# First attention unit's scores and softmax among the last column's products; mask copies by ScalarE

## The chip, the core and the metric

The kernel runs on one core of one Trainium2 chip, alone. The metric is the device time of one execution in microseconds (us). Five engines work side by side, each through its own instruction queue in order: TensorE (PE; its weight loads are listed as PEld), VectorE (DVE), ScalarE (ACT), GpSimd (POOL) and SyncE (SP), which here only issues DMAs. Where two of them share a buffer, one waits for the other.

## What is computed

One step of a hybrid layer. A prompt of 1024 tokens and 8 sample tokens go through one input projection, whose columns feed three groups: a sparse attention group (NSA: compressed, selected and window branches, 8 query heads, 2 key heads), an RWKV-7 recurrence, and cross-attention into 256 memory rows. The parts that matter here:

```
q_raw, kv_raw, g_raw, z_nsa, u_rw, z_rw, q_mem, z_mem = split_in(rms_norm(hp, ln_g[l]) @ w_in[l])
...
s = jnp.where(mask, s.astype(jnp.float32), -jnp.inf)     # masked_softmax
p = jnp.exp(s - m)
return p / jnp.maximum(jnp.sum(p, axis=-1, keepdims=True), 1e-30)
...
cat = jnp.concatenate([o_nsa * silu(z_nsa), o_rw * silu(z_rw), o_mem * silu(z_mem)], axis=-1)
return cat @ w_out
```

With 16 selected blocks of 64 rows in a prompt of 1024, the selected branch is full causal attention; the window branch is limited to 512 rows.

## The kernel before

**Three phases** follow each other in `run`. Phase 1 makes the transposed input `h` (as two parts, high and low, for precision: every product is three matmuls), multiplies it with the columns of `w_in`, 128 columns at a time, and fills the gaps of the RWKV recurrence with those products. Phase 2 does the prompt's attention, with the sample's work between. Phase 3 is the output projection.

**The end of phase 1.** `columns` makes one column block after another, each in two halves of the tokens (H = 0 in pieces of 256 and 264 columns of PSUM, then H = 1 with 512). Eight steps of three matmuls (`p_pr`) make a piece. The last blocks are gate columns: `do_z` takes tanh on ScalarE and a product on VectorE into `zt`, and SP stores it to `z_d`. While these products run, `mix` places other work between them: `keys_ahead` (keys transposed into `kh`, `kl`, and the queries of tile 7), `prompt_cmp` (the compressed keys) and `mem_turn` (memory rows), until `mem_product` multiplies the memory rows (`p_mo`, stored as `mkv`). The last column block comes behind `mem_product`.

**`prompt_cmp`** loads a table of masks, `c_am`, into slot 4 of a pool of eight 4 KB slots, and GpSimd copies it into `bmask` and `cmask` (L1313 to L1318). Then the rows `px` are transposed on TensorE (`p_xt`) and copied by ScalarE into `pxt` (L1340). `pxt` lies in slot 4 too. So the first `pxt` copy cannot start before the last copy out of `c_am` is done. In GpSimd's queue the copies stand behind two DMA issues of the RWKV output (`y_d<-y_c`, L1040).

**Phase 2** goes over units (i, g, hp): query tile i from 7 down, key head g, a pair of heads hp. `attn_scores` makes, for each branch b and head h, the scores on TensorE (`p_s`, two PSUM buffers), adds the mask and takes the maximum in one VectorE instruction (L1478, writes `p` and `nm`), exponentiates on ScalarE (L1485, with the sum), takes a reciprocal on VectorE (`fac`), and scales by it and by the gate on GpSimd (L1516). `attn_turn` transposes the weights `p` (`p_pT`, copied to `pt` by ScalarE and VectorE in turn), and `attn_out` multiplies them with the values (`p_o`). Unit n's transposes and products stand on TensorE with the scores of the units ahead and with pieces of other work: `attn_cmp` (`p_sc`, `pcq`) and `q_stack` (`qhl`, `p_q`).

**What sets the order.** Instructions are recorded in the order of the code, and a scheduler orders them by engine with priorities; work recorded under `high_priority` can move ahead. `InOrder` chains TensorE's matmuls, with a new chain at the start of each phase. A buffer of a pool that lies over an older one waits for the older one's readers: the tiles `p` of phase 2 lie over tiles of phase 1.

Of the kernel before, what the change touches and what calls it, by code (L numbers as in the profile page):

```python
# [10 lines left out]
F32 = mybir.dt.float32  # L11
# [10 lines left out]
NS = 8  # L22
# [25 lines left out]
def bc(ap, shape):  # L48
    return ap.to_broadcast(shape)
# [64 lines left out]
class Step:  # L114
# [357 lines left out]
    def phase1(self):  # L472
# [9 lines left out]
        with ExitStack() as ctx:  # L482
            P = lambda name, bufs, **k: ctx.enter_context(tc.tile_pool(name=name, bufs=bufs, reuse_waits="tile", **k))
            self.small = P("small", 2)
            self.hp = P("hp", 1)
            self.ev = P("ev", 1)
            self.wr = P("wr", 2)
            self.wp = P("wp", 2)
            rctx = ctx.enter_context(ExitStack())
            PR = lambda name, bufs: rctx.enter_context(tc.tile_pool(name=name, bufs=bufs, reuse_waits="tile"))  # L490
# [5 lines left out]
            self.rp = R("rp", 1)  # L496
            self.ppr = P("ppr", 3, space=PSUM)
            self.ptr = P("ptr", 2, space=PSUM)
            self.pw = P("pw", 3, space=PSUM)
            self.hi, self.lo = ([], []), ([], [])  # L500
# [807 lines left out]
    def prompt_cmp(self):  # L1308
# [3 lines left out]
        nc.sync.dma_start(am[:], I["c_at"][:, 0:504])  # L1312
        G.memset(self.bmask[:], 0.0)  # L1313
        G.memset(self.one[:], 1.0)
        G.tensor_copy(self.bmask[:, 0:128], am[:, 128:256])
        G.tensor_copy(self.bmask[:, 1024:1152], am[:, 0:128])
# [136 lines left out]
    def attn_scores(self, i, g, hp, Ps):  # L1453
# [16 lines left out]
        def weigh(ps, h, b, c0):  # L1470
            x, w = Ps[h, b][:, :n1 - c0], n1 - c0
            if b == 1 and split:
                m = bass.AP(tensor=self.bmask.tensor, offset=self.bmask.offset, ap=[self.bmask.ap[0], [832, 2], [1, 320]])
                halves = lambda t: t.rearrange("p (a c) -> p a c", a=2)
            else:
                m, halves = self.bmask[:, 1152 - w:1152], lambda t: t
            def mask():
                return V.tensor_tensor_reduce(halves(x), halves(ps), m, -1.0, 3.0e38, op0=OP.add, op1=OP.min,  # L1478
                                              accum_out=nm[:, h, b:b + 1])

            self.in_turn(mask) if begin else mask()
            if (hp, b, h) in ((0, 1, 1), (1, 0, 0), (1, 1, 0)):
                while self.held:
                    self.held.pop()()
            e = A.activation(x, x, AF.Exp, scale=-1.0, bias=nm[:, h, b:b + 1], accum_out=sm[:, h, b:b + 1])  # L1485
            if (i, g, hp, b, h) == (7, 0, 1, 0, 0):
                self.exp = e

        begin = (i, g) == (7, 0)
        f = self.small.tile([128, 2, 2], F32, name="fac")  # L1490
        hd = 4 * g + 2 * hp
        for b in range(2):
            c0 = w0 if b else 0
            for h in range(2):
                Ps[h, b] = self.pp.tile([128, 1024 if b == 0 else 640], F32, name="p", tag=f"p{b}")
# [15 lines left out]
            def scale(b=b, w=n1 - c0):  # L1511
                recip = lambda: V.reciprocal(f[:, :, b], sm[:, :, b])  # L1512
                self.in_turn(recip) if begin else recip()
                for h in range(2):
                    x = Ps[h, b][:, :w]
                    nc.gpsimd.tensor_scalar(x, x, f[:, h, b:b + 1], gate[:, hd + h, 1 + b:2 + b], op0=OP.mult, op1=OP.mult)  # L1516

            if begin and (hp, b) != (1, 1):
                self.held.append(scale)
            else:  # L1520
                scale()
# [135 lines left out]
    def phase2(self):  # L1657
        tc, nc, I, O = self.tc, self.nc, self.I, self.O
        with ExitStack() as ctx:
# [4 lines left out]
            self.tk = self.wk  # L1664
            self.pS = P("pS", 2, space=PSUM)
            self.pT = P("pT", 3, space=PSUM)
            self.pO = P("pO", 1, space=PSUM)
            self.pM = Tag(self.pT, "t")
# [11 lines left out]
            P = [{} for _ in units]  # L1680
            self.done, self.tail, self.jobs, self.unit = set(), [], [], 0
            self.held, self.mask = [], None
            gens = self.query_tasks(), self.tile_tasks(), self.sample_tasks(), self.sample_rest()
# [53 lines left out]
            next(start)  # L1737
            step(0)
            for _ in start:
                pass  # L1740
            for j, (n, a, b) in enumerate(groups):
                i, g, hp = units[n]
                self.unit = n
                if a == 0:
                    left = sum(1 for m, _, _ in groups if m == n)
                    if (g, hp) == (0, 0):
                        rate = RATE[i]
                        if i < 7:
# [3 lines left out]
                        if i == 7:  # L1752
                            self.load_z(6)
                        if i > 0 and i < 7:
                            self.load_z(i - 1)
                    pieces = sum(4 if units[m][0] >= 4 else 2 for m in ahead(n))
                    nxt = chain(*(scores(m) for m in ahead(n)))
# [27 lines left out]
    def sample_tables(self):  # L1785
# [6 lines left out]
        for d in range(2):  # L1792
            for s in range(2):
                V.tensor_tensor(t[:, 0:3, d, s], g[:, :, s], bc(cos, [NS, 3, 32]), op=OP.mult)
                V.tensor_tensor(t[:, 4:7, d, s], g[:, :, 1 - s], bc(sin, [NS, 3, 32]), op=OP.mult)
            A.activation(rows[:NS, 384 + 64 * d:448 + 64 * d], self.gains[:NS, 4, :], AF.Copy)
        V.tensor_scalar(t[:, 4:7, :, 0], t[:, 4:7, :, 0], -1.0, None, op0=OP.mult)
        return rows[:NS, 0:896].rearrange("p (k c) -> p k c", k=7)

    def sample_setup(self):  # L1800
# [784 lines left out]
```

## Time and profile before

| | us |
|---|---|
| three timed runs | 929.98, 934.21, 935.8 (median 934.21) |
| the profiled execution's own time | 932.48 |
| its span, first to last instruction | 930.7 |
| TensorE busy in the span | 890.9 (96%) |
| VectorE, ScalarE, GpSimd busy | 645.9, 439.6, 189.9 |

The profile is of one execution. A row of the timeline gives the start, the duration, the engine, the line of the kernel, the operation with output and inputs, and in brackets how long the engine was idle before it and what ended that. A duration overlaps with the next instruction's, since instructions are pipelined: the step from one start to the next is the cost. A row of a table by windows gives, for each engine, the busy time in that stretch, then the granted TensorE clock (1.00 is full), the share of time that the DMA engines were busy, and GB/s.

### The profile page before, as it was taken

How to read it: one execution, taken by the hardware profiler on the slowest of the kernel's cores; microseconds unless marked ns; L12 is line 12 of the kernel's file. 1: busy time of each engine (PE TensorE's matmuls, PEld its weight loads, DVE VectorE, ACT ScalarE, POOL GpSimd, SP SyncE). 2: the span in 40 equal slices, each digit the busy share in tenths (PEclk: the TensorE clock that was granted, in tenths of full speed). 3: DMA queues.
4: the chain of work that ended last, by engine and by line, in shares of the span. 5: the costliest groups of instructions: out<-in, count | busy, mean ns of one | idle time of the engine just before them, and what ended most of it. 6: DMA issues, size and time to landing. Idle time of an engine off the chain costs nothing.

```text
span 930.7 us, 24648 instructions
## 1 busy us (share of the span) xinstructions
PE 890.9 (96%) x9839; PEld 756.6 (81%) x9839; DVE 645.9 (69%) x2002; ACT 439.6 (47%) x1003; POOL 189.9 (20%) x283
## 2 busy tenths in 40 slices
PE   8999999999999999988998999999999998999998
PEld 8998888977878788757986788888887877887976
DVE  7768679954777459945556876666778986548454
ACT  7654324232443233223536577667567776324211
POOL 2000000000000000001103544454445766112010
PEclk9999999999999999999999999999999999999999
DMA  8521314141321204524738413332130027986561
GB/s 281 133 74 35 105 36 121 51 115 48 89 82 53 76 14 133 134 84 121 183 102 231 137 59 120 106 117 66 33 87 13 29 81 209 307 259 213 177 236 48
DMA packets 128298, 107.01 MB, mean 115 GB/s; under 512 B 26385, under 2 KB 113112, under 8 KB 128056
## 3 DMA queue, kind: packets, MB, share of 16 engines
q1 hardware_dynamic: 123096, 93.43, 34.3%
q0 software_dynamic: 3296, 10.75, 3.3%
q8 instruction: 78, 1.28, 0.6%
q10 hardware_dynamic: 1792, 1.26, 0.4%
q14 instruction: 36, 0.29, 0.1%
HBM read 84.72 MB, written 22.78 MB: 116 GB/s over the span
## 4 chain that ended last, share of the span: by engine, by line
PE 67%; DVE 18%; ACT 5%; issue 4%; DMA 3%; POOL 2%; SPq 1%; DVEq 0%; ACTq 0%; POOLq 0%
PE p_pr L86 24%; PE p_out L86 8%; PE p_s L86 5%; PE p_o L86 5%; PE p_pT L86 4%; PE p_pr L306 2%; PE p_hid L86 2%; ACT p L1485 2%; DVE p L1478 2%; DMA wraw<-in_w_in_dram 2%; PE p_it L86 1%; DVE wlo L283 1%; PE p_tk L86 1%; PE p_iy L86 1%; DVE pt L1446 1%
## 5 line engine op out<-in xcount | busy, mean ns | idle before, releaser
L86 PE MATMUL p_pr<-h,whi 128*128 128x512 f32 (+2 forms) x1168 | 282.2, 335 | 2.0 <-DVE zt L318 2.0
L86 PEld LDWEIGHTS p_pr<-h,whi 128*128 128x128 f32 x1168 | 190.2, 190 | 22.1 <-issue 2.8
L86 PE MATMUL p_pr<-h,wlo 128*128 128x512 f32 (+2 forms) x584 | 188.9, 326 | 1.1 <-DVE wlo L283 1.1
L1516 POOL TENSOR_SCALAR p<-p,fac,gates 128x640 f32<-128x640 f32 (+7 forms) x128 | 104.2, 826 | 89.4 <-DVE fac L1512 56.0
L86 PEld LDWEIGHTS p_pr<-h,wlo 128*128 128x128 f32 x584 | 109.8, 189 | 11.3 <-DVE wlo L283 1.5
L1485 ACT ACTIVATE p<-p,nm 128x640 f32<-128x640 f32 (+7 forms) x128 | 93.1, 729 | 40.7 <-DVE nm L1478 37.4
L86 PE MATMUL p_pT<-ident,p 128*128 128x128 f32 x528 | 71.9, 279 | 8.8 <-DVE pt L1446 4.0
L1104 POOL MEMSET w2d<- 128x128 f32 x1 | 0.2, 205 | 376.8 <-PE p_iy L86 376.8
L86 PEld LDWEIGHTS p_pT<-ident,p 128*128 128x128 f32 x528 | 56.6, 140 | 21.6 <-issue 5.9
L86 PE MATMUL p_o<-pt,vs 128*64 128x128 f32 x1056 | 67.9, 276 | 0.4 <-DVE cat L1554 0.4
L86 PE MATMUL p_s<-kh,qs 128*128 128x512 f32 (+3 forms) x191 | 64.8, 352 | 1.8 <-DVE nm L1478 1.6
L1478 DVE CUSTOM_DVE_ANT_0 p<-p_s,bmask 128x512 f32<-128x512 f32 (+7 forms) x96 | 60.6, 661 | 7.6 <-PE p_s L86 6.1
L282 ACT ACTIVATE whi<-wraw 128x1024 fp32r<-128x1024 f32 x34 | 36.0, 1059 | 62.3 <-PE p_pr L86 48.8
L86 PEld LDWEIGHTS p_o<-pt,vs 128*64 128x64 f32 x1056 | 57.0, 137 | 7.7 <-issue 4.2
L283 DVE TENSOR_TENSOR wlo<-wraw,whi 128x1024 fp32r<-128x1024 f32 x33 | 40.3, 1221 | 33.0 <-ACT whi L282 32.9
L86 PE MATMUL p_s<-kl,qs 128*128 128x512 f32 (+3 forms) x192 | 60.4, 334 | 0.0
L1446 DVE COPY pt<-p_pT 128x512 f32<-128x512 f32 (+1 forms) x72 | 48.2, 673 | 11.7 <-PE p_pT L86 11.5
L86 PE MATMUL p_out<-woh,chi 128*128 128x512 f32 x128 | 51.7, 404 | 0.0
L86 PE MATMUL p_out<-woh,clo 128*128 128x512 f32 x128 | 50.2, 392 | 0.4 <-DVE clo L2421 0.4
L86 PE MATMUL p_out<-wol,chi 128*128 128x512 f32 x128 | 49.9, 390 | 0.0
L1444 ACT ACTIVATE pt<-p_pT 128x512 f32<-128x512 f32 (+1 forms) x72 | 41.1, 577 | 14.2 <-PE p_pT L86 13.6
L86 PEld LDWEIGHTS p_s<-kh,qs 128*128 128x128 f32 x191 | 36.1, 189 | 5.5 <-DVE nm L1478 3.0
(546 smaller groups left out, 1779.5 us busy)
## 6 DMA issues: line engine op xcount, KB each, us to landing
wraw<-in_w_in_dram SPq DMA_DIRECT2D x34, 512.0 KB
pg<-in_c_pool_dram SPq DMA_DIRECT2D x32, 256.0 KB
pg<-in_c_pool_dram SPq DMA_DIRECT2D x48, 128.0 KB
x<-in_x_prompt_dram SPq DMA_DIRECT2D x8, 512.0 KB
z_d<-zt SPq DMA_DIRECT2D x16, 256.0 KB
cat<-z_d SPq DMA_DIRECT2D x8, 512.0 KB
xres<-in_x_prompt_dram POOLq DMA_DIRECT2D x16, 256.0 KB, 3.6
out_dram<-xres POOLq DMA_DIRECT2D x16, 256.0 KB, 3.0
```

The lines of the kernel that those rows point to most:

```text
L86: self.last = getattr(self.engine, op)(*a, **k)
L282: nc.scalar.activation(hi[:, :, :n], raw[:, :, :n], AF.Copy)
L283: (low or nc.vector).tensor_tensor(lo[:, :, :n], raw[:, :, :n], hi[:, :, :n].bitcast(F32), op=OP.subtract)
L306: self.last_mm = self.pe.matmul(ps[:m, :b - a], w[:, k, :m], h[k][:, a:b], start=(k == 0 and i == 0), stop=(k == 7 and i == 2))
L1104: nc.gpsimd.memset(w2d[:], 0.0)
L1444: nc.scalar.activation(pt[:, :n], ps[:, :n], AF.Copy)
L1446: nc.vector.tensor_copy(pt[:, :n], ps[:, :n])
L1478: return V.tensor_tensor_reduce(halves(x), halves(ps), m, -1.0, 3.0e38, op0=OP.add, op1=OP.min, accum_out=nm[:, h, b:b + 1])
L1485: e = A.activation(x, x, AF.Exp, scale=-1.0, bias=nm[:, h, b:b + 1], accum_out=sm[:, h, b:b + 1])
L1516: nc.gpsimd.tensor_scalar(x, x, f[:, h, b:b + 1], gate[:, hd + h, 1 + b:2 + b], op0=OP.mult, op1=OP.mult)
```

## The change

1. The copies from `c_am` into `bmask` and `cmask` go from GpSimd to ScalarE, and GpSimd clears only the columns of `bmask` that no copy writes.
2. `first_scores` runs the scores and softmax of unit 0, (7, 0, 0), inside the last column block, at the steps given by `AT`. Its PSUM buffers `pS` are opened once the buffers of `ptr` and `pw` are closed, and its four `p` tiles lie in slots 4, 5, 6 and 0, with maxima, sums and factors in unused columns of the tile in slot 6.
3. What follows from it: phase 2 starts with unit 1's scores, `cat6` is loaded at unit 1 (it lies in slot 6), the sample's tables and cleared tiles wait for unit 0's last reciprocal, exponential and scaling, unit 1's first scalings are held in other places, and the pool `ev` (with `zt`) is opened behind `wr` and `wp`.

```diff
+AT = (1, 5, 8, 11)
...
             self.hp = P("hp", 1)
-            self.ev = P("ev", 1)
             self.wr = P("wr", 2)
             self.wp = P("wp", 2)
+            self.ev = P("ev", 1)
...
-            self.ppr = P("ppr", 3, space=PSUM)
-            self.ptr = P("ptr", 2, space=PSUM)
-            self.pw = P("pw", 3, space=PSUM)
+            self.ppr = P("ppr", 3, space=PSUM, side="right")
+            pctx = ctx.enter_context(ExitStack())
+            PP = lambda name, bufs: pctx.enter_context(tc.tile_pool(name=name, bufs=bufs, reuse_waits="tile", space=PSUM))
+            self.ptr = PP("ptr", 2)
+            self.pw = PP("pw", 3)
...
-            self.mix(work, chain(self.columns(cols[EARLY:-1]), self.mem_product(), self.columns(cols[-1:])))
+            self.mix(work, chain(self.columns(cols[EARLY:-1]), self.mem_product()))
+            pctx.close()
+            self.pS = self.kctx.enter_context(tc.tile_pool(name="pS", bufs=2, reuse_waits="tile", space=PSUM))
+            self.first_scores(self.columns(cols[-1:]))
+
+    def first_scores(self, fill):
+
+        self.held, self.mask = [], None
+        self.P0 = {}
+        gen = self.attn_scores(7, 0, 0, self.P0)
+        for n, _ in enumerate(fill):
+            if n in AT:
+                next(gen, None)
+        for _ in gen:
+            pass
+        self.lasts = [x.ins for x in (self.r_last, self.e_last, self.g_last)]
...
-        G.memset(self.bmask[:], 0.0)
+        G.memset(self.bmask[:, 128:1024], 0.0)
         G.memset(self.one[:], 1.0)
-        G.tensor_copy(self.bmask[:, 0:128], am[:, 128:256])
-        G.tensor_copy(self.bmask[:, 1024:1152], am[:, 0:128])
+        A.activation(self.bmask[:, 0:128], am[:, 128:256], AF.Copy)
+        A.activation(self.bmask[:, 1024:1152], am[:, 0:128], AF.Copy)
         self.cmask = self.kt.tile([128, 248], F32R, name="cmask")
-        G.tensor_copy(self.cmask[:], am[:, 256:504])
+        A.activation(self.cmask[:], am[:, 256:504], AF.Copy)
...
+        early = (i, g, hp) == (7, 0, 0)
+        begin = (i, g, hp) == (7, 0, 1)
+        if early:
+            for (h, b), j in zip(((0, 0), (1, 0), (0, 1), (1, 1)), (4, 5, 6, 0)):
+                Ps[h, b] = self.slot(j, [128, 1024], F32, f"p{j}")
+            nm, sm, f = (Ps[0, 1][:, c:c + 4].rearrange("p (h b) -> p h b", b=2) for c in (1000, 1004, 1008))
+        else:
+            nm, sm, f = (self.small.tile([128, 2, 2], F32, name=x) for x in ("nm", "sm", "fac"))
...
-            start = chain(scores(0), scores(1))
-            for k in range(6):
+            start = scores(1)
+            for k in range(2):
                 next(start)
-                if k in (0, 1, 4):
-                    step(0)
+                step(0)
             pts = turn(*groups[0])
-            step(0)
-            next(start)
+            for k in range(2):
+                step(0)
+                next(start)
             step(0)
...
-                V.tensor_tensor(t[:, 0:3, d, s], g[:, :, s], bc(cos, [NS, 3, 32]), op=OP.mult)
-                V.tensor_tensor(t[:, 4:7, d, s], g[:, :, 1 - s], bc(sin, [NS, 3, 32]), op=OP.mult)
+                with self.tc.issue_after(self.lasts[0]):
+                    V.tensor_tensor(t[:, 0:3, d, s], g[:, :, s], bc(cos, [NS, 3, 32]), op=OP.mult)
+                    V.tensor_tensor(t[:, 4:7, d, s], g[:, :, 1 - s], bc(sin, [NS, 3, 32]), op=OP.mult)
```

Where the instructions stand. On GpSimd before, the copies out of `c_am` stand behind the two stores of the recurrence and the clearing of `bmask`:

```order
L1040 DMA y_d<-y_c 128x256 x2
L1313 MEMSET bmask 128x1152
L1314 MEMSET one 128x1
L1318 CAST cmask<-c_am 128x248
L1315 CAST bmask<-c_am 128x128
L1316 CAST bmask<-c_am 128x128
```

On ScalarE after, they stand between the last gate piece and the first `pxt` copy, which reuses slot 4:

```order
L318 ACTIVATE zt<-p_pr 128x256
L318 ACTIVATE zt<-p_pr 128x264
L1333 ACTIVATE bmask<-c_am 128x128
L1334 ACTIVATE bmask<-c_am 128x128
L1336 ACTIVATE cmask<-c_am 128x248
L1358 ACTIVATE pxt_6349<-p_xt 128x512
L1312 ACTIVATE kh_6225<-p_k_6375 64x2x256
```

The three copies have left GpSimd's queue and stand in ScalarE's; the rows around them keep their order.

On TensorE in the second half of the last column block (`p_pr_7063`), after, with buffer numbers: `p_s_7083` is unit 0's last score tile, `p_s_7149` is unit 1's first, and it lies in the PSUM buffer of unit 0's third tile (`p_s_7067`):

```order
L87 MATMUL p_pr_7063<-h01_3_813,wlo_6982 128x512
L87 MATMUL p_s_7083<-kh0_6225,qs_6604 128x128
L84 MATMUL p_s_7149<-kh0_6225,qs_6604 128x512
L87 MATMUL p_s_7149<-kl0_6226,qs_6604 128x512
L87 MATMUL p_s_7149<-kh1_6228,qs_6604 128x512
L87 MATMUL p_s_7149<-kl1_6229,qs_6604 128x512
L87 MATMUL p_s_7083<-kl0_6226,qs_6604 128x128
L87 MATMUL p_s_7083<-kh1_6228,qs_6604 128x512
L87 MATMUL p_s_7083<-kl1_6229,qs_6604 128x512
L87 MATMUL p_pr_7063<-h01_4_897,whi_6981 128x512
```

Before, no `p_s` of either unit stood ahead of the end of the column block; now unit 1's first scores stand in the middle of it as well, ahead of half of the piece's matmuls.

On VectorE after, directly behind the memory rows' last instruction (`mkv`); the rows ISA are the mask instructions and the reading of their maxima, `p_6999` to `p_7002` the four tiles in the slots:

```order
L1502 ISA p_6999,p_7001<-p_s,bmask 128x1024
L1502 ISA p_7001 128x1
L319 SCALAR_TENSOR_TENSOR zt<-zt,p_pr 128x256
L1502 ISA p_7000,p_7001<-p_s,bmask 128x1024
L1502 ISA p_7001 128x1
L1533 RECIPROCAL p_7001<-p_7001 128x2
L319 SCALAR_TENSOR_TENSOR zt<-zt,p_pr 128x264
L1502 ISA p_7001<-p_s,bmask 128x640
L1502 ISA p_7001 128x1
L1502 ISA p_7002,p_7001<-p_s,bmask 128x640
L1502 ISA p_7001 128x1
L1533 RECIPROCAL p_7001<-p_7001 128x2
```

Before, the gate pieces `zt` and the sample's tables `s_in` stood at this place and unit 0's masks behind them; now the masks alternate with the gate pieces, and the tables come behind the last row shown, ahead of unit 1's first mask.

More of the change, by code (lines that the diff above doesn't have):

```diff
@@ L1461, in attn_scores @@
         gate = self.gates[:, i, :].rearrange("p (h b) -> p h b", b=3)
-        nm = self.small.tile([128, 2, 2], F32, name="nm")
-        sm = self.small.tile([128, 2, 2], F32, name="sm")
+        early = (i, g, hp) == (7, 0, 0)
[6 more added lines that the diff above has]
+            nm, sm, f = (self.small.tile([128, 2, 2], F32, name=x) for x in ("nm", "sm", "fac"))
         def scores(ps, q, b, c0, c1):
@@ L1481, in weigh @@
             self.in_turn(mask) if begin else mask()
[L1482 to L1485, printed above, removed]
+            while self.held and h == 0:
+                self.held.pop()()
+            e = self.e_last = A.activation(x, x, AF.Exp, scale=-1.0, bias=nm[:, h, b:b + 1], accum_out=sm[:, h, b:b + 1])
             if (i, g, hp, b, h) == (7, 0, 1, 0, 0):
                 self.exp = e
-        begin = (i, g) == (7, 0)
-        f = self.small.tile([128, 2, 2], F32, name="fac")
         hd = 4 * g + 2 * hp
@@ L1493, in attn_scores @@
             c0 = w0 if b else 0
-            for h in range(2):
+            for h in range(0 if early else 2):
                 Ps[h, b] = self.pp.tile([128, 1024 if b == 0 else 640], F32, name="p", tag=f"p{b}")
@@ L1512, in scale @@
                 recip = lambda: V.reciprocal(f[:, :, b], sm[:, :, b])
-                self.in_turn(recip) if begin else recip()
+                if begin:
+                    self.in_turn(recip)
+                else:
+                    self.r_last = recip()
                 for h in range(2):
                     x = Ps[h, b][:, :w]
-                    nc.gpsimd.tensor_scalar(x, x, f[:, h, b:b + 1], gate[:, hd + h, 1 + b:2 + b], op0=OP.mult, op1=OP.mult)
-            if begin and (hp, b) != (1, 1):
+                    self.g_last = nc.gpsimd.tensor_scalar(x, x, f[:, h, b:b + 1], gate[:, hd + h, 1 + b:2 + b], op0=OP.mult, op1=OP.mult)
+            if begin and b == 0:
                 self.held.append(scale)
@@ L1664, in phase2 @@
             self.tk = self.wk
-            self.pS = P("pS", 2, space=PSUM)
-            self.pT = P("pT", 3, space=PSUM)
-            self.pO = P("pO", 1, space=PSUM)
+            self.pT = P("pT", 3, space=PSUM, side="right")
+            self.pO = P("pO", 1, space=PSUM, side="right")
             self.pM = Tag(self.pT, "t")
@@ L1679, in phase2 @@
                 groups += [(n, a, min(a + size, total)) for a in range(0, total, size)]
-            P = [{} for _ in units]
+            P = [{} if n else self.P0 for n in range(len(units))]
             self.done, self.tail, self.jobs, self.unit = set(), [], [], 0
-            self.held, self.mask = [], None
             gens = self.query_tasks(), self.tile_tasks(), self.sample_tasks(), self.sample_rest()
@@ L1751, in phase2 @@
                             until(2, "win")
-                        if i == 7:
-                            self.load_z(6)
                         if i > 0 and i < 7:
                             self.load_z(i - 1)
+                    if n == 1:
+                        self.load_z(6)
                     pieces = sum(4 if units[m][0] >= 4 else 2 for m in ahead(n))
@@ L1793, in sample_tables @@
             for s in range(2):
-                V.tensor_tensor(t[:, 0:3, d, s], g[:, :, s], bc(cos, [NS, 3, 32]), op=OP.mult)
-                V.tensor_tensor(t[:, 4:7, d, s], g[:, :, 1 - s], bc(sin, [NS, 3, 32]), op=OP.mult)
-            A.activation(rows[:NS, 384 + 64 * d:448 + 64 * d], self.gains[:NS, 4, :], AF.Copy)
+                with self.tc.issue_after(self.lasts[0]):
+                    V.tensor_tensor(t[:, 0:3, d, s], g[:, :, s], bc(cos, [NS, 3, 32]), op=OP.mult)
+                    V.tensor_tensor(t[:, 4:7, d, s], g[:, :, 1 - s], bc(sin, [NS, 3, 32]), op=OP.mult)
+            with self.tc.issue_after(self.lasts[1]):
+                A.activation(rows[:NS, 384 + 64 * d:448 + 64 * d], self.gains[:NS, 4, :], AF.Copy)
         V.tensor_scalar(t[:, 4:7, :, 0], t[:, 4:7, :, 0], -1.0, None, op0=OP.mult)
@@ L1812, in sample_setup @@
         for x in (qb, q64, qmb, self.gr):
-            G.memset(x[:], 0.0)
+            with tc.issue_after(self.lasts[2]):
+                G.memset(x[:], 0.0)
         sums = self.slot(1, [128, 1024], F32, "s_in1")[:, 0:128]
```

## The prediction

> **What bounds the kernel.** The first lines of the page say that TensorE is busy for 890.9 of 930.7 us, so only time in which it waits, or runs at a lower clock, can be won. The change leaves the count of matmuls as it is; its two parts touch two places where TensorE waits. I read them in the order of waits of TensorE, its timeline there, then the rows of the engines that it waits for. First the stretch around 430 us, in the table of waits (total us, times, longest) and in the timeline of TensorE:
>
> ```profile
> PE 890.9 (96%) x9839; PEld 756.6 (81%) x9839; DVE 645.9 (69%) x2002; ACT 439.6 (47%) x1003; POOL 189.9 (20%) x283
> ...
> PE p_xt L86 <- ACT pxt L1340: 3.0, 1, 3.0
> ...
> 426.08 0.60 PE L86 MATMUL p_xt<-ident,px 128*128 128x128 f32 x4
> 428.06 0.39 PE L86 MATMUL p_pr<-h,wlo 128*128 128x512 f32 x1
> 431.45 1.12 PE L86 MATMUL p_xt<-ident,px 128*128 128x128 f32 x4 [3.00 <-ACT pxt L1340]
> 432.74 1.89 PE L86 MATMUL p_pc<-w1s,peT 128*2 128x128 f32 x32 [0.17 <-DVE peT L1073]
> 434.56 0.76 PE L86 MATMUL p_pr<-h,whi 128*128 128x512 f32 x2
> ```
>
> One wait of 3.00 us, the longest at this place. Why ScalarE was late stands in the rows of GpSimd, ScalarE and VectorE:
>
> ```profile
> 428.32 0.55 POOL L1040 DMA_DIRECT2D y_d<-y_c  x1 [1.09 <-DVE y_c L1038]
> 428.87 1.08 POOL L1313 MEMSET bmask<- 128x1152 bf16 x1
> 430.47 0.30 POOL L1316 CAST bmask<-c_am 128x128 bf16<-128x128 f32 x1
> ...
> 425.49 0.39 ACT L317 ACTIVATE zt<-p_pr 128x264 f32<-128x264 f32 x1 [2.92 <-PE p_pr L86]
> 430.80 0.60 ACT L1340 ACTIVATE pxt<-p_xt 128x512 f32<-128x512 f32 x1 [4.93 <-POOL bmask L1316]
> 431.30 0.58 ACT L1294 ACTIVATE kh<-p_k 64x512 fp32r<-64x512 f32 x1
> ...
> 431.91 0.68 DVE L1295 TENSOR_TENSOR kl<-p_k,kh 64x512 fp32r<-64x512 f32 x1 [4.13 <-ACT kh L1294]
> 432.51 0.17 DVE L1073 COPY peT<-p_pe 128x32 f32<-128x32 f32 x1
> ```
>
> ScalarE stood idle for 4.93 us because GpSimd's copies came behind the stores of the recurrence. The tables by windows show what the idle array cost afterwards (behind DVE, ACT and POOL: granted clock, DMA share, GB/s):
>
> ```profile
> 431.40:432.80 1.40, 1.18 (x8) 0.78 (x12) 0.78 (x2) 1.13 (x3) 0.00 (x0) 0.50 0.52 187
> 432.80:434.60 1.80, 1.80 (x33) 0.97 (x33) 0.69 (x1) 1.01 (x2) 0.00 (x0) 0.50 0.00 0
> 434.60:440.00 5.40, 5.40 (x33) 4.47 (x30) 2.53 (x6) 1.93 (x4) 0.00 (x0) 0.99 0.24 50
> ```
>
> The clock was 0.50 from 431.4 to 434.6. Now the second place, where phase 2 begins:
>
> ```profile
> 495.00:500.00 5.00, 4.08 (x23) 3.10 (x22) 3.73 (x8) 3.15 (x10) 0.00 (x0) 1.00 0.96 266
> 500.00:505.00 5.00, 3.87 (x20) 2.56 (x20) 4.60 (x13) 4.28 (x10) 3.19 (x3) 1.00 0.76 231
> 505.00:510.00 5.00, 4.17 (x31) 3.10 (x28) 3.37 (x11) 3.90 (x9) 3.44 (x5) 1.00 1.08 300
> 510.00:515.00 5.00, 3.95 (x42) 3.32 (x42) 4.96 (x10) 3.19 (x8) 5.00 (x6) 1.00 1.14 359
> ```
>
> TensorE is busy for 16.07 of these 20 us: 3.93 us is the most that a perfect second part could take from them.
>
> **Part one, the mask copies.** On ScalarE three copies of 128, 128 and 248 columns come in behind `zt` at 425.49. The nearest rows:
>
> ```profile
> 463.06 0.27 ACT L1235 ACTIVATE ck<-p_k 128x128 fp32r<-128x128 f32 x1
> 482.31 0.38 ACT L375 ACTIVATE nr_sq<-p_mo 128x256 f32<-128x256 f32 x1
> ```
>
> 2 x 0.27 + 0.38 = 0.92. So `zt` ends at 425.88, the copies at 426.8, `pxt` at 427.4, `kh` at about 427.9, `kl` at 428.6, `peT` at 428.8. GpSimd keeps a shorter clearing that nobody waits for before 480. TensorE ends the product before its wait at 428.06 + 0.39 = 428.45 and goes straight on: four transposes, about 0.5 by the row at 426.08, then `p_pc` at 428.95, where `peT` is just ready. `p_pc` took 434.56 - 432.74 = 1.82 at clock 0.50. Its cost at full clock isn't shown: at best half, 0.91, at worst the same 1.82. The weight loads filled 0.97 of its 1.80, so I put it nearer the half, at 1.1. The next product starts at 430.05 instead of 434.56: **4.5 us gained**, between 3.8 and 4.7. From there on every row of the chain to 470 (keys, copies, weight splits) is behind this one, so all of it moves.
>
> The Trainium skill, "TensorE: Matmul & The Clock Gate", section "Part 1: The HAM clock gate (the "warmup" mystery)", says that the array falls to half clock after an idle window of about 3.4 us and comes back after as long a busy one. By that figure a wait of 3.00 us need not cost any clock, and the gain would be 3.8; the window rows above show that here it did.
>
> **Part two, unit 0's scores.** Four groups of scores move into the last column block. They cost TensorE the same there; what they could win is the chain behind the block. In its rows the block starts at 482.53 and the scores follow at 494.57:
>
> ```profile
> 482.53 0.40 PE L86 MATMUL p_pr<-h,whi 128*128 128x256 f32 x2
> 494.57 0.39 PE L83 MATMUL p_s<-kh,qs 128*128 128x512 f32 x1
> 495.50 0.28 PE L86 MATMUL p_sc<-cmask 128*128 128x256 f32 x1
> 513.26 1.97 PE L86 MATMUL p_o<-pt,vs 128*64 128x128 f32 x32
> ...
> 488.20 0.42 DVE L384 TENSOR_TENSOR mkv<-mkv,gains 128x256 f32<-128x256 f32 x1
> 491.52 0.25 DVE L1794 TENSOR_TENSOR s_in<-gains,rope 8x96 f32<-8x96 f32 x1 [2.89 <-DMA out_dram<-mkv]
> 495.41 0.69 DVE L318 SCALAR_TENSOR_TENSOR zt<-zt,p_pr 128x512 f32<-128x512 f32 x1 [1.95 <-ACT zt L317]
> 496.96 1.22 DVE L1478 CUSTOM_DVE_ANT_0 p<-p_s,bmask 128x1024 f32<-128x1024 f32 x1 [0.87 <-DMA z_d<-zt]
> 499.92 0.82 DVE L1478 CUSTOM_DVE_ANT_1 p<-p_s,bmask 128x640 f32<-128x640 f32 x1
> ...
> 498.24 1.14 ACT L1485 ACTIVATE p<-p,nm 128x1024 f32<-128x1024 f32 x1
> 501.81 4.11 POOL L1516 TENSOR_SCALAR p<-p,fac,gates 128x1024 f32<-128x1024 f32 x4 [13.18 <-DMA z_d<-zt]
> ```
>
> The first score and the `p_sc` behind its group of four show 0.93 us for a wide group; a narrow one lies between 0.58 (by its 640 of 1024 columns) and that, I take 0.75. The block's 12.04 us hold 8 steps of 520 columns and 8 of 512, so a step of the second half is 0.7. I walk the changed order with these durations, in the clock of before (part one moves all alike), up to the first `p_o`, 513.26 before.
>
> *Masks against gate pieces.* VectorE is free for a mask when `mkv` is done, at 488.62, or 488.2 since a gate piece no longer stands ahead. First mask to exponential is 1.28 (496.96 to 498.24). But the two engines now hand over in turn: mask 488.2, exponential 489.5, `zt` on ScalarE behind it 490.6 (0.39, as at 425.49), `zt` on VectorE 491.05, second mask 491.45, exponential 492.75, `zt` 493.9 and 494.3, third mask 494.7 to 495.5 (0.82, as at 499.92).
>
> *TensorE in the block.* With three groups inside it reaches the fourth at 482.53 + 12.04 - 2.8 + 2.6 = 494.4. There unit 1's scores wait for the buffer of the third mask, to 495.5, with half a piece of products queued behind them: 1.1 us of waiting that did not exist. They and the rest of the group take 1.6; the last four steps end at 499.9.
>
> *Behind the block.* Fourth mask 497.1, exponential 498.4, reciprocal 499.4; then six small table instructions that before ran in idle time (from 491.52 on; 1.0 together), unit 1's mask at 500.4, `zt` at 501.6 to 502.2. TensorE does `p_sc` and scores to 501.5 and waits 0.7 for the PSUM bank of `zt`. The transposes of unit 0 have their weights ready, but each bank needs a copy or an addition that stands behind unit 1's masks and exponentials: some 0.4, 1.0 and 0.9 of waits. I arrive at `p_o` at 512.3, **1.0 earlier**.
>
> *The load of the queries.* In SP's queue `q` now stands behind `cats`, which waits for the landing of `z_d`. What a landing takes, in the chain of work:
>
> ```profile
> 497.10 4.63 DMA z_d<-zt
> ...
> 493.68 0.46 SPq L320 DMA_DIRECT2D z_d<-zt  x1
> 495.15 0.43 SPq L1363 DMA_DIRECT2D q<-q_d  x1
> ...
> 504.44 0.40 ACT L1369 ACTIVATE qhl<-q 128x256 fp32r<-128x256 f32 x1
> ```
>
> `z_d` is issued at about 495.3. With 3.3 us to its landing (the mask at 496.96 waited for the store of 493.68), 0.6 for the issues and 3.3 for `q`, it is there at 502.5, and ScalarE wants it at 502.8; with 4.63 for both, at 505.2. ScalarE has `pcq`, exponentials and copies behind it, so lateness counts in full: 0 to 2.4 us, I take 0.8. **Part two then gives 0.2**, between -1.4 and 3.9. Near nothing, since VectorE has as much work as before between 488 and 513 and idles as long, in other places.
>
> The same Trainium skill page, section "A second HAM failure mode: psum-queue depth-cycling", speaks against this part: short pauses between groups of matmuls can let the clock swing. One fall for 3.2 us would cost 1.6. Here the clock was 1.00 in the window from 500, with TensorE busy for 3.87 of 5.
>
> **Does it last?** After 515 us the waits of TensorE are few and none is for a DMA; the largest total is this, so an earlier start stays earlier:
>
> ```profile
> PE p_pT L86 <- DVE pt L1446: 2.9, 5, 0.9
> ```
>
> **The sum.** 4.5 + 0.2 = 4.7 from the profiled execution's 932.48 gives 927.8; from the median of 934.21 it gives 929.5. I take 928.5.
>
> **Rivals.** *Both parts pay* (chance 0.17): ScalarE and VectorE hand over faster than I walked, the 3.93 us go as well. For it: GpSimd's scaling, 501.8 before, is done for half of unit 0 by 497. Against it: the order of VectorE. 932.48 - 4.5 - 3.9 = 924.1.
>
> *The masks' part does not arrive* (0.13): the copies write the tile that GpSimd clears, and if ScalarE still waited for that (428.87 + 0.8), `pxt` would start at 430.6; or another engine is late by as much, a key row's load for instance. Against it: the cleared columns and the copied ones no longer overlap. 0 to 1 us gained: 932.
>
> *Slower* (0.07): the load of `q`. If the DMA engines are so full at 495 to 505 (shares of 0.96 and 0.76 before, now with three cache loads ahead of `z_d` in the queue) that the two landings take 7 us each, `q` lands at 509.9, 7.1 after it is wanted: 932.48 - 4.5 - 1.0 + 7.1 = 934.1. From 508.3 on it eats the whole gain. Against it: before, `q` was issued at 495.15 and used at 504.44 without a wait.
>
> *The clock swings* (0.03): 927.8 + 1.6 = 929.4.
>
> My forecast has 0.60. The range, 924 to 933, reaches over the bounds of both parts and leaves out the slower case and half of the case in which both pay. A change of 1% is 9.3 us, about what a measurement of this kernel can tell from none; only the lower half of the case in which both pay reaches it: faster by over 1% 0.10, within 1% 0.88, slower 0.02.
>
> **What the profile after would show.** Right: no wait of TensorE for `pxt`, a clock of 1.00 there, `p_pc` some 4 us earlier; the last column block longer by 5 us, with a wait of `p_s` for `nm` in its middle of about 1 us; first `p_o` about 4.7 us earlier than 513.26, hence near 508.5. Wrong: a wait for `pxt` or a key load that remains near 427; waits of 3 us or more for `qhl` or `q`; a low clock anywhere between 480 and 515; or an end that comes earlier by much less than the first `p_o`.

## The result, and the profile after

The kernel after took 927.32 us (median; 923.18 to 929.95) where the kernel before took 932.69 (928.98 to 936.55) beside it. The ratio is **0.9937, with a 95% interval of 0.992 to 0.9955**: 5 to 6 us faster, less than 1%. The profiled execution took 927.17 us, with a span of 925.4.

The first place of the change, in TensorE's timeline of the kernel after:

```profile
422.17 0.60 PE L87 MATMUL p_xt<-ident,px 128*128 128x128 f32 x4
...
426.97 0.60 PE L87 MATMUL p_xt<-ident,px 128*128 128x128 f32 x4
427.87 1.05 PE L87 MATMUL p_pc<-w1s,peT 128*2 128x128 f32 x32 [0.30 <-DVE peT L1091]
428.85 0.73 PE L87 MATMUL p_pr<-h,whi 128*128 128x512 f32 x2
...
476.14 0.40 PE L87 MATMUL p_pr<-h,whi 128*128 128x256 f32 x2
```

The transposes at 426.97 wait for nothing: the 3.00 us for `pxt` are gone, and `p_pc` takes 1.05 instead of 1.89. ScalarE's timeline shows why; its copies stand right behind `zt`, and `pxt` starts at 425.39, where it had started at 430.80:

```profile
424.56 0.30 ACT L1333 ACTIVATE bmask<-c_am 128x128 bf16<-128x128 f32 x1
424.76 0.30 ACT L1334 ACTIVATE bmask<-c_am 128x128 bf16<-128x128 f32 x1
424.96 0.40 ACT L1336 ACTIVATE cmask<-c_am 128x248 fp32r<-128x248 f32 x1
425.39 0.60 ACT L1358 ACTIVATE pxt<-p_xt 128x512 f32<-128x512 f32 x1
```

The windows (the granted clock stands third from the end of a row) show full clock at this place, and, much later, a stretch at lower clock that the profiled execution of before did not have:

```profile
428.40:431.40 3.00, 3.00 (x35) 2.46 (x26) 1.81 (x5) 0.97 (x2) 0.29 (x3) 1.00 0.69 239
...
780.00:784.00 4.00, 4.00 (x40) 3.26 (x39) 1.04 (x7) 1.90 (x3) 3.26 (x7) 0.66 1.07 378
```

The second place, in TensorE's timeline again:

```profile
488.64 0.50 PE L84 MATMUL p_s<-kh,qs 128*128 128x512 f32 x1 [1.13 <-DVE p L1502]
...
495.75 0.38 PE L87 MATMUL p_sc<-cmask 128*128 128x256 f32 x1 [1.11 <-DVE zt L319]
...
497.46 0.66 PE L87 MATMUL p_pT<-ident,p 128*128 128x128 f32 x4 [0.47 <-DVE pcq L1422]
498.93 0.66 PE L87 MATMUL p_pT<-ident,p 128*128 128x128 f32 x4 [0.82 <-DVE pcq L1422]
500.36 0.66 PE L87 MATMUL p_pT<-ident,p 128*128 128x128 f32 x4 [0.77 <-ACT pt L1462]
...
505.74 1.97 PE L87 MATMUL p_o<-pt,vs 128*64 128x128 f32 x32
...
509.77 0.66 PE L87 MATMUL p_pT<-ident,p 128*128 128x128 f32 x4 [0.60 <-DVE pt L1464]
...
512.61 0.60 PE L87 MATMUL p_pT<-ident,pcq 128*128 128x128 f32 x4
```

and in the kernel before the first of the `p_xt`, two waits for `wlo` (a part of the weights) at the memory product and in the last column block, and the transposes of `pcq`:

```profile
423.38 0.60 PE L86 MATMUL p_xt<-ident,px 128*128 128x128 f32 x4
...
479.86 0.50 PE L86 MATMUL p_mo<-wlo,mhi 128*128 128x512 f32 x1 [0.40 <-DVE wlo L1180]
483.36 0.38 PE L86 MATMUL p_pr<-h,wlo 128*128 128x256 f32 x1 [0.43 <-DVE wlo L283]
...
519.37 0.60 PE L86 MATMUL p_pT<-ident,pcq 128*128 128x128 f32 x4
```

With these rows the difference of the two spans, 5.3 us, can be followed through the program. The start of a row after, less that of the same row before: -1.21 at the first `p_xt` (422.17 - 423.38), where the change has done nothing yet; -5.71 at the product behind `p_pc` (428.85 - 434.56); -6.39 at the start of the last column block (476.14 - 482.53); -7.52 at the first `p_o`; -6.76 at the transposes of `pcq`; -5.3 at the end. So **4.50 us** were won between the first `p_xt` and the product behind `p_pc`. Another 0.68 were won up to the last column block: 0.40 of it is the wait at 479.86, which this trace doesn't have; e8, the same program in another execution, has 0.23 of it, so it comes and goes. Up to the first `p_o` came 1.13 more, of which 0.43 is the wait at 483.36; all five traces without part two have such a wait (0.16 to 0.43), and none of the nine with it shows one. Of the 1.13, 0.76 were given back within 7 us, because a group of transposes waits 0.60 for a copy of VectorE. The last 1.46 went later, 1.1 of it in the stretch of half clock at 780. The next section shows the 1.21 and what was lost at 780 to be scatter.

### The profile page after: what moved, and what is told of

Its sections match the earlier page's. It is cut to its first block, busy times and chain, and to the rows that moved or that the text cites. A ratio compares the mean times of both kernels' runs of the same rounds, so it can differ in the third digit from the quotient of the medians.

```text
span 925.4 us, 24648 instructions
## 1 busy us (share of the span) xinstructions
PE 888.4 (96%) x9839; PEld 757.6 (82%) x9839; DVE 646.1 (70%) x2002; ACT 440.1 (48%) x1006; POOL 188.9 (20%) x280
## 4 chain that ended last, share of the span: by engine, by line
PE 71%; DVE 17%; ACT 6%; issue 3%; DMA 1%; POOL 1%; SPq 0%; DVEq 0%; ACTq 0%; POOLq 0%
PE p_pr L87 26%; PE p_out L87 9%; PE p_s L87 5%; PE p_o L87 4%; PE p_pT L87 4%; PE p_hid L87 4%; ACT p L1508 3%; DVE p L1502 3%; PE p_pr L307 2%; PE p_tk L87 1%; DMA wraw<-in_w_in_dram 1%; DVE pt L1464 1%; PE p_it L87 1%; PE p_iy L87 1%; PE p_z L87 1%
## 5 line engine op out<-in xcount | busy, mean ns | idle before, releaser
L1540 POOL TENSOR_SCALAR p<-p,fac,gates 128x640 f32<-128x640 f32 (+7 forms) x124 | 100.1, 819 | 77.4 <-DVE fac L1533 57.5
L1508 ACT ACTIVATE p<-p,nm 128x640 f32<-128x640 f32 (+7 forms) x124 | 89.2, 720 | 41.8 <-DVE nm L1502 38.0
```

What stands on the lines that cost most here:

```text
L1508: e = self.e_last = A.activation(x, x, AF.Exp, scale=-1.0, bias=nm[:, h, b:b + 1], accum_out=sm[:, h, b:b + 1])
L1540: self.g_last = nc.gpsimd.tensor_scalar(x, x, f[:, h, b:b + 1], gate[:, hd + h, 1 + b:2 + b], op0=OP.mult, op1=OP.mult)
```

## The experiments

Three lengths are read from each trace, so that what other places of the program did does not enter: **A**, from the first `p_xt` to the product behind `p_pc`; **B**, from the first product of the last column block to the first `p_o`; **C**, from the same product to the transposes of `pcq`. The last column gives the times (us) before 900 from which the granted clock was 0.5 for some 3.4 us (x2: twice as long); each ratio has its 95% interval.

| kernel | ratio to before | A | B | C | half clock at |
|---|---|---|---|---|---|
| before | 1 | 11.18 | 30.73 | 36.84 | 274, 322, 431 |
| after | 0.9937 (0.992 to 0.9955) | 6.68 | 29.60 | 36.47 | 274, 322, 779 |
| e1_copies | 0.995 (0.993 to 0.9969) | 6.67 | 31.62 | 37.86 | 274, 322, 377, 507 |
| e2_scores | 0.9996 (0.9981 to 1.0012) | 11.19 | 31.09 | 37.20 | 427, 502, 782 |
| e3_copies_first | 1.0002 (0.9987 to 1.0018) | 9.31 | 30.51 | 36.60 | 275, 374 |
| e4_unit1_kept | 0.9927 (0.9912 to 0.9943) | 6.66 | 31.56 | 37.67 | 319, 497 x2 |
| e5_slots_swapped | 0.9928 (0.9902 to 0.9954) | 6.67 | 30.53 | 36.64 | 321 |
| e6_copies_first_2 | 0.9973 (0.9956 to 0.999) | 10.13 | 29.77 | 35.85 | 320, 430 |
| e7_early_groups | 0.9906 (0.9879 to 0.9934) | 6.71 | 29.69 | 35.80 | 273, 321, 498 |
| e8_change_2 | 0.9919 (0.9894 to 0.9944) | 6.69 | 32.73 | 38.84 | 273, 321, 499 x2 |
| e9_filled_pause | 0.9897 (0.9874 to 0.9919) | 6.67 | 27.48 | 34.46 | 320 |
| e10_filled_more | 0.9913 (0.9892 to 0.9933) | 6.66 | 30.49 | 36.59 | 274, 321 |
| e11_change_filled | 0.9915 (0.9901 to 0.993) | 6.67 | 29.82 | 36.69 | 273, 321 |
| e12_filled_pause_2 | 0.9906 (0.9891 to 0.9921) | 6.67 | 27.59 | 34.58 | none |

**Each part alone.** The theory: part one carries nearly the whole gain, by taking away one wait and the half clock behind it. The rival: both parts pay.

```diff
# e1_copies: before, with part one (the second of the three copies alike)
-        G.memset(self.bmask[:], 0.0)
+        G.memset(self.bmask[:, 128:1024], 0.0)
...
-        G.tensor_copy(self.bmask[:, 0:128], am[:, 128:256])
+        A.activation(self.bmask[:, 0:128], am[:, 128:256], AF.Copy)
...
-        G.tensor_copy(self.cmask[:], am[:, 256:504])
+        A.activation(self.cmask[:], am[:, 256:504], AF.Copy)
# e2_scores: after, with these lines as they were before
```

> Part one alone. Theory (the copies carry the gain): TensorE's row behind p_pc comes about 4.4 us earlier against its row at 425, the clock stays at 1.00 there, and the end moves with it: ratio near 0.9953. Rival (the scores carry a good part): the gain at the end is 3 us or less, ratio 0.997 or more.

> Part two alone. Theory: the wait of 3.00 us for pxt and the half clock are there as before; the block of the last columns is about 4.8 us longer, the first p_o comes about 1 us earlier, and the end between 0 and 1 us earlier: ratio 0.999 to 1.000. Rival (both parts pay): 3 us or more, ratio 0.997 or less.

Part one alone shortens A from 11.18 to 6.67 us and gives 0.995. Part two alone leaves A at 11.19 and gives 0.9996, which no interval here tells from nothing. Its wait for `pxt` and its half clock are the old ones (TensorE, e2_scores):

```profile
427.39 1.12 PE L87 MATMUL p_xt<-ident,px 128*128 128x128 f32 x4 [3.13 <-ACT pxt L1358]
428.68 1.89 PE L87 MATMUL p_pc<-w1s,peT 128*2 128x128 f32 x32 [0.17 <-DVE peT L1091]
```

The rival's 3 us for part two is ruled out: its interval ends at 0.9981, 1.8 us.

**A shorter wait, twice.** GpSimd makes the copies ahead of its clearing:

```diff
# e3_copies_first and e6_copies_first_2: before, with
-        G.memset(self.bmask[:], 0.0)
-        G.memset(self.one[:], 1.0)
         G.tensor_copy(self.bmask[:, 0:128], am[:, 128:256])
...
         G.tensor_copy(self.cmask[:], am[:, 256:504])
+        G.memset(self.bmask[:, 128:1024], 0.0)
+        G.memset(self.one[:], 1.0)
```

> GpSimd still makes the copies, but ahead of its clearing (1.08 us) instead of behind it. The copies end about 1.1 us earlier, so TensorE's wait for pxt falls from 3.00 to about 1.9 us. If the half clock is the price of the length of the wait, it is gone too: gain 1.1 + 1.4 = 2.5 us, ratio 0.9973. If the clock falls at any wait here, or by chance of when it comes, the gain is the wait alone: 1.1 us, ratio 0.9988.

> GpSimd's copies ahead of its clearing, a second sample, since the trace of the first showed 1.9 us gained at the place and its timed runs nothing. If those runs were scatter of the clock at other places: a wait of about 2.1 us at full clock again, and a ratio near 0.9975. If a wait of 2.1 us brings the half clock in some executions: half clock in this trace, or a ratio that stays over 0.999.

TensorE in the first, then in the second:

```profile
429.39 0.66 PE L86 MATMUL p_xt<-ident,px 128*128 128x128 f32 x4 [2.09 <-ACT pxt L1340]
430.68 1.06 PE L86 MATMUL p_pc<-w1s,peT 128*2 128x128 f32 x32 [0.63 <-DVE peT L1073]
```

```profile
428.40 0.66 PE L86 MATMUL p_xt<-ident,px 128*128 128x128 f32 x4 [2.11 <-ACT pxt L1340]
429.69 1.89 PE L86 MATMUL p_pc<-w1s,peT 128*2 128x128 f32 x32 [0.63 <-DVE peT L1073]
```

One program, the same wait within 0.02 us, and the clock fell in one of two executions: A is 9.31 in the one and 10.13 in the other. So the half clock isn't the price of a length of wait alone; a wait gives it a chance, and the last section shows on what that hangs. The intervals of the two ratios, 1.0002 and 0.9973, hardly overlap: how much of the shorter wait reaches the end is not settled by them.

**The wait without the copies.** Is it the copies on ScalarE that help, or only that `pxt` stops waiting for a slot that GpSimd still reads?

```diff
# e5_slots_swapped: before, with
-        xt = self.slot(4 + e, [128, 4, 2, 128], F32, f"pxt{e}")
+        xt = self.slot(5 - e, [128, 4, 2, 128], F32, f"pxt{e}")
```

> The kernel before, with the two tiles pxt in each other's slots: the first no longer lies where the copies of GpSimd read, so it needs no copy to be done, and GpSimd copies as late as before. If the wait for the slot is what part one takes away: no wait of TensorE for pxt at 430, clock 1.00, 4.4 us earlier, ratio 0.9953, with no copy on ScalarE. If it was GpSimd being late for something else as well: the third pxt, now in the copies' slot, holds up ScalarE, keys and p_pc behind it, and 2 us or less are gained, ratio 0.998 or more.

On ScalarE, where `pxt` stands for both tiles in turn:

```profile
425.15 0.58 ACT L1340 ACTIVATE pxt<-p_xt 128x512 f32<-128x512 f32 x1
427.49 0.59 ACT L1294 ACTIVATE kh<-p_k 64x512 fp32r<-64x512 f32 x1 [1.75 <-DVE kl L1295]
429.33 0.60 ACT L1340 ACTIVATE pxt<-p_xt 128x512 f32<-128x512 f32 x1 [1.26 <-POOL bmask L1316]
```

The third `pxt` does wait for the copies, until 429.33, but nothing that TensorE needs by then stands behind it: A is 6.67, and the ratio 0.9928. The wait is the whole of part one. One changed index gives what the three copies on ScalarE give.

**Inside the second place.** Unit 1's first scores are kept behind the block by starting phase 2's order of TensorE from the last matmul of phase 1; then the groups are put earlier as well:

```diff
# e4_unit1_kept: after, with
+            last = self.te.last
             self.te = nc.tensor
...
-            self.te = InOrder(tc, nc.tensor, None)
+            self.te = InOrder(tc, nc.tensor, last)
# e7_early_groups: the same, and
-AT = (1, 5, 8, 11)
+AT = (1, 2, 5, 7)
```

> The change, with unit 1's first scores kept behind the last column products; VectorE then also makes the last gate piece ahead of unit 1's mask. If TensorE's order inside the block and at its end sets the first p_o: the waits of 1.13 us in the block and 1.11 us for the gate piece are gone, and the first p_o comes 1.2 us (0.6 to 2.2) earlier than with the change, ratio to before near 0.9925. If the handing over between VectorE and ScalarE sets it: the waits move to the transposes, and the first p_o moves by less than 0.4 us.

> The change with unit 1's scores kept behind the block and the groups of unit 0 put after steps 1, 2, 5 and 7 instead of 1, 5, 8 and 11. If the handing over of masks and exponentials behind the block sets the first p_o: all four masks are done before the block ends, the waits for the gate piece and the second pcq shrink to under 0.5 us, the first p_o comes 2.5 us (1.5 to 3.5) earlier than with the change, ratio to before near 0.991. If what the block wins is lost again behind it: first p_o within 0.7 us of the change's, ratio near 0.9935.

e4's row of `p_sc`, and its transposes; then e7's transposes and the scores behind them:

```profile
492.91 0.39 PE L87 MATMUL p_sc<-cmask 128*128 128x256 f32 x1 [1.38 <-DVE zt L319]
...
496.66 0.80 PE L87 MATMUL p_pT<-ident,p 128*128 128x128 f32 x4 [1.62 <-DVE pcq L1422]
```

```profile
497.25 0.66 PE L87 MATMUL p_pT<-ident,p 128*128 128x128 f32 x4 [1.62 <-DVE pcq L1422]
498.41 1.11 PE L87 MATMUL p_pT<-ident,p 128*128 128x128 f32 x4 [0.50 <-ACT pt L1462]
...
500.17 0.63 PE L87 MATMUL p_s<-kl,qs 128*128 128x512 f32 x1
```

The wait of 1.13 us in the block is gone in both, that for `zt` in e7 alone; what was waited for at the second `pcq` grew to 1.62 in both. And here both traces show half clock: a score of 512 columns takes 0.63. So the first `p_o` came no earlier than in the change (B: 31.56 and 29.69 against 29.60). The expectations failed there, though the ratios are no worse than the change's.

**The change again.**

> The change itself, a second sample beside the others. Theory: the shift against the kernel before is 4.4 us between 423 and 440 and about 1 us more at the first p_o; half clock appears for some 3.3 us at two to four of the places 272, 320, 376, 500 and 780 us, not the same ones as in the first trace; ratio 0.9937. Rival: the places are the same, and so belong to the change.

ScalarE, then TensorE, then the windows:

```profile
496.97 0.42 ACT L1387 ACTIVATE qhl<-q 128x256 fp32r<-128x256 f32 x1 [0.94 <-DMA q<-q_d]
```

```profile
498.17 0.66 PE L87 MATMUL p_pT<-ident,p 128*128 128x128 f32 x4 [1.51 <-DVE pcq L1422]
499.64 1.12 PE L87 MATMUL p_pT<-ident,p 128*128 128x128 f32 x4 [0.82 <-DVE pcq L1422]
501.07 1.12 PE L87 MATMUL p_pT<-ident,p 128*128 128x128 f32 x4 [0.31 <-ACT pt L1462]
```

```profile
498.00:502.00 4.00, 2.70 (x13) 2.07 (x14) 2.95 (x7) 2.45 (x5) 1.82 (x3) 0.59 0.91 291
502.00:506.00 4.00, 4.00 (x18) 3.51 (x18) 3.21 (x9) 0.99 (x2) 1.45 (x3) 0.55 1.02 314
```

The same program as after, and another execution: ScalarE waits 0.94 us for the load of `q`, which in the first trace had landed in time, the wait for `pcq` grows from 0.47 to 1.51, and half clock holds for about 6.8 us. B is 32.73, longer than before's 30.73, while A is 6.69 again. The first trace was a lucky one at this place. The late load isn't needed for the fall: in e2_scores `q` was not late, TensorE's waits were those of the first trace within 0.1 us (1.22, 1.07, 0.46, 0.82 and 0.77), and half clock came at 502. The half clock at 780, in turn, is missing here, and e2_scores has it: it comes and goes between executions. The places at 274 and 322 are before's too, and so no part of the change.

**Filling the pauses.** Four of the five traces that have part two unfilled show half clock between 497 and 506 (all but the first); of the five without it one does, at 507. If it comes from TensorE's sparse work there, matmuls that nobody reads should hold the clock. `FILL` says how many stand ahead of each group of unit 0's transposes:

```diff
# e9_filled_pause and e12_filled_pause_2: e7_early_groups, with FILL = (0, 0, 3, 0)
+    def fill(self, n):
...
+            PE.matmul(self.dm[:], self.qs[7][:, 0, :], self.kh[0][:, 0, :], start=True, stop=True)
...
+            if self.dm is not None and j < 8:
+                self.fill(FILL[j // 2])
             out.append(self.pt_copy(lambda j: src[j], "b", len(src)))
# e10_filled_more: the same with (0, 2, 5, 2);  e11_change_filled: after, with (0, 1, 1, 1)
```

> The early groups, with three matmuls of 512 columns that nobody reads (some 0.7 us, into a PSUM bank that is free until the first p_o) ahead of the third group of transposes, where TensorE waited 1.62 us; every other engine's order is unchanged. If the half clock near 500 comes from sparse work of TensorE there, it appears in fewer executions: no half clock between 490 and 510 in this trace, the scores behind the transposes take 0.23 us each instead of up to 0.6, and the first p_o comes some 0.9 us earlier than in the early groups without filling. If 0.7 us is too little or the sparse work isn't the cause: half clock for about 3.3 us there again.

> The same with two, five and two such matmuls ahead of the second, third and fourth group of transposes (2.1 us), which also moves the softmax of the compressed keys ahead by some places on VectorE. If sparse work is the cause: no half clock between 490 and 510; the first p_o up to 0.9 us earlier than in the early groups, or equal where the filling runs over the waits by as much. Rival: half clock there again, first p_o later by what the filling runs over, 0.5 us or more.

> The change as it is (groups after steps 1, 5, 8 and 11, unit 1's scores inside the block), with one matmul of 512 columns that nobody reads ahead of each of the second, third and fourth group of transposes (0.23 us each, inside waits of 0.47, 0.82 and 0.77 us). If breaking up the pauses is enough against the half clock: none between 490 and 510 here, and a ratio near 0.992. If the waits of over 1 us that stay (1.1 in the block, 1.1 for the gate piece) bring it: half clock there again, first p_o 1 to 2 us later than in the change's first trace, ratio 0.994.

> The early groups with the filled pause, a second sample. If its gain is real: full clock between 490 and 510 again, first p_o 7 to 8 us behind the row that follows p_s of the fourth group by as much as in the first sample, and a ratio of 0.990 (0.988 to 0.992), below the change's 0.9919 and 0.9937. If the first sample was a lucky execution: half clock there, and a ratio of 0.992 or more.

TensorE in e9, then in e12 with its windows, then in e11:

```profile
494.12 0.94 PE L88 MATMUL dm<-kh,qs 128*128 128x512 f32 x3
495.82 0.66 PE L88 MATMUL p_pT<-ident,p 128*128 128x128 f32 x4 [0.76 <-DVE pcq L1426]
...
502.52 1.97 PE L88 MATMUL p_o<-pt,vs 128*64 128x128 f32 x32
```

```profile
493.25 0.66 PE L88 MATMUL p_pT<-ident,p 128*128 128x128 f32 x4 [0.88 <-DVE pcq L1426]
...
499.93 1.97 PE L88 MATMUL p_o<-pt,vs 128*64 128x128 f32 x32
```

```profile
492.00:496.00 4.00, 2.62 (x17) 1.92 (x16) 2.47 (x5) 3.10 (x8) 2.46 (x3) 1.00 1.00 347
496.00:500.00 4.00, 4.00 (x26) 3.05 (x27) 3.56 (x11) 3.45 (x9) 1.85 (x2) 1.00 1.06 340
```

```profile
495.58 0.48 PE L88 MATMUL dm<-kh,qs 128*128 128x512 f32 x1
496.52 0.66 PE L88 MATMUL p_pT<-ident,p 128*128 128x128 f32 x4 [0.46 <-DVE pcq L1426]
```

None of the four filled traces has half clock there. e9 and e12 have B of 27.48 and 27.59, 2.1 to 2.2 us shorter than e7's, where 0.9 was expected; their C is 1.2 to 1.3 us shorter. Their ratios, 0.9897 and 0.9906, lie below the change's two, with intervals that overlap but for e9's and the first of the change. But e7, the same without filling, has 0.9906 as well: the traces show what the filling does at its place, the timed runs don't show that it pays. e12's expectation gives a distance of 7 to 8 us that was put wrongly; from unit 1's first score to the first `p_o` it is 12.16 us in e9 (502.52 - 490.36) and 12.26 in e12. e10 loses its gain again: its moved softmax puts an exponential ahead of a copy that TensorE then waits for, 1.6 us (B 30.49). In e11 full clock holds, though the two waits of over 1 us are still there; that speaks against the rival in its expectation, but one trace doesn't settle it, since the change's own first trace held it too. Its C, 36.69, is as long as before's (36.84). So even with the clock held, these traces show no gain of part two as it stands. **The early groups with the filled pause** have the shortest B and C, and are the version to take by the traces.

Half clock also makes a part of the scatter ahead of 423: e2 and e12, which have none at 274 and 322, reach the first `p_xt` 4.07 and 5.19 us earlier than before does, with the same order of TensorE's instructions up to there. It is not all of it: the six traces with half clock at 274 and 322 and nowhere else ahead of 423 reach it between 420.97 (e11) and 423.38 (before). The 1.21 us of the first trace are inside this.

## Why the prediction was right, point by point

- **Part one, predicted 4.5 (3.8 to 4.7); measured 4.50.** All ten traces with the wait taken away have A between 6.66 and 6.71, against 11.18. The steps hold: no wait for `pxt`, `p_pc` at full clock. That the number fits to 0.01 us is luck, three small errors that cancel. The four transposes began 4.80 us behind the first `p_xt` where the sum has 5.07 (in large part because it went by the duration of the product ahead, 0.39, where the step to the next row is 0.23: 426.97 - 426.74). `p_pc` came 0.90 behind them instead of 0.5, with a wait for `peT` of 0.30. And `p_pc` took 0.98 to the next row (428.85 - 427.87), where 1.1 was chosen. The three copies take 0.83 from 424.56 to `pxt` at 425.39, where 0.92 was put.
- **Part two, predicted 1.0 up to the first `p_o`, less 0.8 for the late `q`.** In the first trace 1.13 was won and `q` was not late; 0.76 was then given back behind the first `p_o`, a step that the prediction didn't have (it let an earlier start last). Net 0.37, where 0.2 was put. That 1.13 fits the 1.0 is partly luck: 0.43 of it is a wait for `wlo` that the walk didn't count, and the order of before, at full clock there, shows a B from 30.73 down to 29.77 (e6), so these traces don't tell 1.13 from scatter. In the second trace `q` was late, by 0.94, in none of the other eight traces with part two. The mechanism, near nothing in sum, was right; the late load belongs to some executions only.
- **The walk through the block.** Predicted waits: 1.1 for the third mask's buffer, 0.7 for the bank of `zt`, and 0.4, 1.0 and 0.9 at the transposes. Measured: 1.13, 1.11, and 0.47, 0.82 and 0.77. Only the second was mis-sized, by 0.41; the block ended 0.51 us sooner than walked (493.00 - 476.14 = 16.86 us behind its start, where the walk has 499.9 - 482.53 = 17.37), which made up for it. e2 and e11 repeat the waits of the block and of `zt` (1.22 and 1.07, 1.21 and 1.12).
- **"Does it last?"** Where no half clock differs, nearly: the 6.76 us of lead at the transposes of `pcq` stay within 1 us up to 775. At 780 the trace lost 1.1 us, to a fall of the clock that comes in some executions only. So one of the signs of being wrong, an end that comes earlier by much less than the first `p_o` (5.3 against 7.52), did show, for reasons outside the sum.
- **The clock as a rival, chance 0.03.** This is the one estimate that the runs overturn. Half clock at the second place showed in four of five traces of unfilled part two, and made e8's C 2.4 us longer than the first trace's, together with the late `q`. A low clock between 480 and 515 was another of the signs of being wrong. The row that the prediction relied on (full clock from 500, busy for 3.87 of 5) was one execution of another order.
- **Both parts pay, 0.17.** Not in the change: e2_scores gives 0.9996. The 3.93 us of waiting were partly there to win, by the lengths B and C of e9 and e12, but only with other places for the groups and with the clock held.

The forecast of 928.5 thus stands on part one; part two added about nothing to it, in some executions by a gain that a fall of the clock takes back.

## What to carry to other kernels

Before moving work to another engine to take away a wait, look for what is waited for: here it was a slot that two tiles shared, and another slot did as well as the other engine. Where TensorE has several short waits close together, count a fall of the clock as a likely cost and not as an accident, and try matmuls that nobody reads in the longest pause; here they shortened the stretch in two traces, and the timed runs couldn't tell whether the whole gained. One trace at full clock doesn't show that a place is safe. Compare lengths between rows inside one trace; two spans of one kernel here differ by more than the change is worth.

## What was not expected of the hardware

Read in windows of 0.2 us, every stretch in the table's last column sums to 3.41 or 3.42 us at half clock, or to 6.83: 3.42 in the kernel before at 431, 3.41 in e2 at 427, 502 and 782, 6.83 in e4 at 497 and in e8 at 499. They come in units of one length, in some executions and not in others.

Their starts lie on a grid: inside one trace any two are a whole number of 3.413 us apart, to 0.01 us. In the kernel before they are at 274.23, 322.01 and 431.24, 14 and 46 units behind the first; in the kernel after the one at 779.27 is 148 units behind the one at 274.10. (In traces with few or no falls the first rise to full clock gives the grid; in the kernel after it is at 7.86, 78 units ahead of 274.10.) Cut along this grid, the 14 traces have, ahead of 900 us, 16 windows at full clock in which TensorE was busy for under 0.50 of the time, and half clock followed all 16. At 0.50 to 0.63 it followed 15 of 44 windows, above 0.63 none of 3561. So whether a wait costs the clock hangs on how the grid cuts it. The wait of 2.1 us lies in one window in e6, and in e3 it is shared by two; the chain of short waits, alike within 0.1 us, was cut badly in e2 and less so in the kernel after. Windows on the grid of e6, then two of e3, then e2, then after (PE's busy time is the second number):

```profile
426.24:429.65 3.41, 0.71 (x5) 0.42 (x4) 0.78 (x2) 1.63 (x4) 2.37 (x7) 1.00 0.95 281
```

```profile
425.33:428.74 3.41, 1.98 (x9) 1.19 (x7) 1.39 (x4) 0.00 (x0) 2.16 (x6) 1.00 0.66 161
428.74:432.15 3.41, 2.12 (x38) 1.60 (x39) 1.71 (x4) 2.75 (x5) 0.93 (x3) 1.00 0.61 212
```

```profile
498.87:502.28 3.41, 1.51 (x10) 0.84 (x8) 3.19 (x7) 2.36 (x7) 1.38 (x2) 1.00 0.93 264
```

```profile
495.96:499.38 3.42, 2.14 (x17) 1.63 (x16) 2.61 (x7) 2.37 (x7) 1.41 (x2) 1.00 0.92 261
```

Half clock followed the first and the fourth row alone. The filled versions can be read in the same way: wherever a window of 3.41 us is laid between 486 and 512, it holds at least 2.15 us of busy TensorE in e9 and 2.03 in e12, but 1.83 in e11 and 1.61 in e10 at the worst place; e7's window ahead of its half clock had 1.31. So the filled pause takes away the windows under 0.50 wherever the grid lies, and the full clock of e10 may be a lucky cut.

The Trainium skill, "TensorE: Matmul & The Clock Gate", section "Part 1: The HAM clock gate (the "warmup" mystery)", gives 3413 ns for a window of activity that runs freely, without regard to the kernel. The length and the grid agree. But a whole window without work, which the section asks for, is more than these traces had: the emptiest window ahead of half clock still had 0.47 us of busy TensorE (e2, from 423.79).

The same page, section "Part 4: PE-mode transpose", says that transposes don't count as busy in the same way. The stretches near 430 and 500 lie where TensorE makes transposes between waits, and the matmuls that held the clock were no transposes. But a window on the grid of the kernel after that holds little else than transposes (22 of its 25 matmuls, `p_pT`, `p_sv` and `p_yT`) kept full clock, and no half clock followed, so here transposes did count:

```profile
697.35:700.76 3.41, 2.89 (x25) 2.19 (x23) 3.22 (x11) 2.62 (x8) 1.63 (x2) 1.00 0.00 0
```
